# A hybrid mLSTM/attention backbone on one core: the norm's modulated input, its Newton step, its residual, and z in wide matmuls

## The chip, the core and the metric

The kernel runs on one core of a Trainium2 chip. The time is the device time of one execution in microseconds (us). The core's engines have queues of their own and run side by side: TensorE (PE in the profile; PEld are its weight loads), VectorE (DVE), ScalarE (ACT), GpSimd (POOL) and SyncE (SP, which here issues DMAs). Within a queue the order is that of the program; between queues semaphores make an instruction wait for its operands. SBUF is the memory on the chip, PSUM the memory into which TensorE writes.

## What is computed

Two layers over 512 tokens (256 context tokens, then 256 latent ones) of width 1024. Each layer is FFN, token mixer (mLSTM in layer 0, windowed attention in layer 1), FFN. Each of the six sub-layers takes an input that is modulated by a scale and a shift from a conditioning vector, and is followed by a LayerNorm of the weighted sum of the residual and the gated output:

```python
def layer_norm(x, g, b):
    mu = xf.mean(-1, keepdims=True)
    var = jnp.mean(jnp.square(xf - mu), -1, keepdims=True)
    return (xf - mu) * lax.rsqrt(var + LN_EPS) * g + b
def modulate(s, m, slot):
    return s * (1 + m[..., 3 * slot + 1, :]) + m[..., 3 * slot, :]
def residual_post_norm(s, y, gate, weight, g, b):
    return layer_norm(ALPHA * s + weight * gate * y, g, b)
...
xm, z = jnp.split(u @ w_up, 2, axis=-1)         # mLSTM: u is 512 x 1024, z is 512 x 2048
h = jax.nn.sigmoid(z) * h                       # the gate on the mLSTM's output
```

Everything is fp32 in and out.

## The kernel before, in words

*Products.* A product of two fp32 matrices is made of three TensorE products of a high and a low part: each operand is split into `hi`, its rounding to the matmul's own type, and `lo`, what is left, and `mm3` adds hi·hi, hi·lo and lo·hi in PSUM. Weights come from HBM as raw fp32 tiles of 1 MB and less; ScalarE rounds them (`w`, L375) and VectorE or GpSimd subtracts (L376). The sub-layer's input is kept as `uh` and `ul`, eight tiles of 128 features x 512 tokens each.

*Layout.* The residual is `as`, eight SBUF tiles of 128 features x 512 tokens. The tokens are two halves: C0 (columns 0 to 255) and C1 (256 to 511).

*The norm between two sub-layers.* While a sub-layer's output is evicted (L761: `as = y*gate + as`), `Norm.add` accumulates the sum and the sum of squares (`acc`, L107 and L108). `Norm.finish` runs once a half: small matmuls against ones give mean and mean square (`stat`); variance plus epsilon goes through GpSimd's pow and one Newton step (L138 to L141, `rsqrt`, L794 to L799: `ln` tiles of 128x2); GpSimd subtracts the mean from the eight `as` tiles (L145); TensorE spreads the 1/sigma of each token over all partitions into a PSUM tile `rstd`; VectorE multiplies each `as` tile by it in place (L168); `modulate` makes `uh` (ScalarE, L566), `uf` (VectorE, L567) and `ul = uf - uh` (VectorE, L568); and GpSimd later turns `as` into the next residual, scale and shift by `ag` (L174). `Norm` with two halves runs four times: FFN to mLSTM (the first norm, from about 390 us), mLSTM to FFN (the second, from about 810), FFN of layer 0 to FFN of layer 1 (the third, from about 1196) and FFN to attention (the fourth, from about 1573). It runs once with one half, attention to the last FFN (from about 1720). The norm after the last FFN is another class and stays as it is.

*z.* In the mLSTM, z is made with tokens on the partitions: for each of eight column blocks `q` of 256, `tok_major` runs, for each of four tiles of 128 tokens, eight feature tiles x 3 matmuls of 128x128 by 128x256. Two token tiles share a PSUM tile of 128x512, which ScalarE evicts with a tanh (L951) and which is then stored.

*What sets the order.* TensorE's and SyncE's orders are written out by a planner: tasks are generators that yield a delay or an event, `drive` always runs the first task that is due on a clock `k.T`, which matmuls advance by their modelled time. Its constants (LAT, SOLO, RY in ns) say how long after one step of the norm the next is put into the program: LAT[0] and LAT[1] before the statistics of the first and second half, LAT[2] (SOLO with one half) between statistics and `rstd`, LAT[3] and LAT[4] from `rstd` to the first use of `u`, RY from the modulated input to the residual's rescale. VectorE's, ScalarE's and GpSimd's orders come from a scheduler, in which `high_priority` moves an instruction forward.

## Time and profile before

| | |
|---|---|
| median of 3 runs | 1941.97 us (1941.0 to 1946.05) |
| the profiled execution's own time | 1937.41 us |
| its span, first to last instruction | 1935.6 us |
| mean granted TensorE clock | 0.989 |
| TensorE busy | 1881.0 us, 97 % |
| VectorE, ScalarE, GpSimd busy | 69 %, 42 %, 19 % |
| z matmuls (128x256) | 768 |

How to read the rows that follow. A row of a group reads: line, engine, operation, written tile <- read tiles, shape, count | busy us in all, mean ns of one | idle us of the engine just before them, and what ended most of it. A row of a timeline reads: start us, us, engine, line, operation, tiles, count, and in brackets the idle time before it and what ended that. A row of the waits reads: waiting engine, its tile and line <- the engine, tile and line that ended the wait: us in all, times, longest. A row of the chain reads: start, us, engine, tile, line, count. A row of windows reads: window, its length, then PE, PEld, DVE, ACT and POOL busy with counts, then the granted TensorE clock, the DMA share and GB/s.

### The profile page before, as it was taken

How to read it: one execution, taken by the hardware profiler on the slowest of the kernel's cores; microseconds unless marked ns; L12 is line 12 of the kernel's file. 1: busy time of each engine (PE TensorE's matmuls, PEld its weight loads, DVE VectorE, ACT ScalarE, POOL GpSimd, SP SyncE). 2: the span in 40 equal slices, each digit the busy share in tenths (PEclk: the TensorE clock that was granted, in tenths of full speed). 3: DMA queues.
4: the chain of work that ended last, by engine and by line, in shares of the span. 5: the costliest groups of instructions: out<-in, count | busy, mean ns of one | idle time of the engine just before them, and what ended most of it. 6: DMA issues, size and time to landing. Idle time of an engine off the chain costs nothing.

```text
span 1935.6 us, 28837 instructions
## 1 busy us (share of the span) xinstructions
PE 1881.0 (97%) x10946; PEld 1610.6 (83%) x10946; DVE 1339.4 (69%) x2424; ACT 819.3 (42%) x1521; POOL 366.6 (19%) x397
## 2 busy tenths in 40 slices
PE   7999999999999999989999999999999999989997
PEld 5888888897889977978888889888888888789997
DVE  4976677986664689777776679776633468966565
ACT  3443233246555563343323333433233335745452
POOL 2000000570012344450000025400000256140000
PEclk9999999999999999999999999999999999999999
DMA  9654454435343464335455434454432224126652
GB/s 318 218 203 166 153 194 160 136 120 185 96 150 115 134 215 142 109 116 182 154 180 174 158 136 142 148 185 147 152 107 87 94 69 131 45 66 198 194 164 99
DMA packets 227435, 287.55 MB, mean 149 GB/s; under 512 B 7968, under 2 KB 197536, under 8 KB 227296
## 3 DMA queue, kind: packets, MB, share of 16 engines
q1 hardware_dynamic: 226384, 282.75, 44.1%
q0 software_dynamic: 912, 2.95, 0.4%
q8 instruction: 86, 1.41, 0.3%
q14 instruction: 53, 0.43, 0.1%
HBM read 269.94 MB, written 15.73 MB: 148 GB/s over the span
## 4 chain that ended last, share of the span: by engine, by line
PE 56%; DVE 3%; POOL 1%; issue 1%; ACT 1%; DVEq 0%; POOLq 0%; ACTq 0%
PE gv L294 31%; PE y L294 19%; PE q L294 1%; PE s L294 1%; DVE ul L568 1%; PE o L294 1%; PE stat L294 0%; DVE uf L567 0%; PE pT L301 0%; PE msum L294 0%; PE h L294 0%; POOL as L145 0%; DVE as L168 0%; ACT e L1386 0%; PE swap L294 0%
## 5 line engine op out<-in xcount | busy, mean ns | idle before, releaser
L294 PE MATMUL gv<-uh,w 128*128 128x512 f32 (+1 forms) x2944 | 799.7, 358 | 11.5 <-DVE w L376 5.5
L375 ACT ACTIVATE w<-raw 128x512 fp32r<-128x512 f32 x636 | 395.7, 630 | 692.7 <-PE gv L294 395.6
L376 DVE TENSOR_TENSOR w<-raw,w 128x512 fp32r<-128x512 f32 x604 | 433.7, 723 | 299.1 <-ACT w L375 296.9
L294 PEld LDWEIGHTS gv<-uh,w 128*128 128x128 f32 x2944 | 527.1, 191 | 97.9 <-DVE w L376 5.7
L294 PE MATMUL gv<-ul,w 128*128 128x512 f32 (+1 forms) x1472 | 525.1, 357 | 1.8 <-DVE ul L568 1.8
L294 PE MATMUL y<-hh,w 128*128 128x512 f32 (+1 forms) x1600 | 405.6, 342 | 0.0
L493 DVE SCALAR_TENSOR_TENSOR macc<-mraw,cs,macc 128x512 f32<-128x512 f32 x448 | 331.7, 785 | 41.0 <-DMA mraw<-in_mod_w 32.0
L294 PEld LDWEIGHTS gv<-ul,w 128*128 128x128 f32 x1472 | 281.0, 191 | 40.5 <-DVE ul L568 2.4
L294 PEld LDWEIGHTS y<-hh,w 128*128 128x128 f32 x1600 | 277.9, 190 | 37.7 <-issue 3.2
L294 PE MATMUL y<-hl,w 128*128 128x512 f32 (+1 forms) x800 | 272.2, 340 | 0.0
L88 POOL TENSOR_TENSOR as<-as,shift 128x512 f32<-128x512 f32 (+1 forms) x40 | 57.6, 1475 | 889.0 <-ACT shift L86 889.0
L294 PEld LDWEIGHTS y<-hl,w 128*128 128x128 f32 x800 | 151.7, 190 | 17.6 <-issue 0.7
L761 DVE SCALAR_TENSOR_TENSOR as<-y,gate,as 128x256 f32<-128x256 f32 x184 | 78.9, 476 | 36.3 <-PE y L294 36.2
L294 PE MATMUL z<-w,uh 128*128 128x256 f32 x512 | 94.1, 285 | 0.0
L294 PE MATMUL xm<-uh,w 128*128 128x512 f32 (+1 forms) x320 | 91.3, 359 | 0.0
L677 DVE TENSOR_TENSOR sg<-sg,gv 128x512 f32<-128x512 f32 (+1 forms) x88 | 54.0, 618 | 52.9 <-PE gv L294 48.5
L294 PE MATMUL y<-hnh,w 128*128 128x512 f32 (+1 forms) x320 | 85.2, 350 | 0.7 <-DVE as L761 0.7
L376 POOL TENSOR_TENSOR w<-raw,w 128x512 fp32r<-128x512 f32 x32 | 45.7, 1429 | 201.9 <-ACT w L375 194.0
L294 PEld LDWEIGHTS z<-w,uh 128*128 128x128 f32 x512 | 79.8, 191 | 2.5 <-issue 2.1
L294 PE MATMUL z<-w,ul 128*128 128x256 f32 x256 | 72.4, 283 | 0.0
L294 PEld LDWEIGHTS xm<-uh,w 128*128 128x128 f32 x320 | 57.8, 195 | 12.2 <-issue 5.0
L558 ACT ACTIVATE hh<-sg 128x512 fp32r<-128x512 f32 (+1 forms) x88 | 50.3, 575 | 37.0 <-DVE sg L677 37.0
(298 smaller groups left out, 2279.3 us busy)
## 6 DMA issues: line engine op xcount, KB each, us to landing
raw<-in_ffn_w_in SPq DMA_DIRECT2D x84, 1024.0 KB, 5.2
mraw<-in_mod_w SPq DMA_DIRECT2D x128, 512.0 KB, 6.1
raw<-in_ffn_w_out SPq DMA_DIRECT2D x48, 768.0 KB, 4.6
raw<-in_ml_w_up SPq DMA_DIRECT2D x15, 1024.0 KB, 5.8
m<-in_mod_w SPq DMA_DIRECT2D x32, 256.0 KB, 6.6
raw<-in_ffn_w_out SPq DMA_DIRECT2D x16, 512.0 KB, 3.4
raw<-in_ml_w_down SPq DMA_DIRECT2D x16, 512.0 KB, 3.9
raw<-in_at_w_qkv SPq DMA_DIRECT2D x6, 1024.0 KB, 5.1
```

The source lines that it names most:

```text
L88: nc.gpsimd.tensor_tensor(out=k.as_[d][:, cols], in0=k.as_[d][:, cols], in1=sh[:, cols], op=ALU.subtract)
L294: k.nc.tensor.matmul(out, lhsT=lhsT, rhs=rhs, start=start, stop=stop, skip_group_check=True, **kw)
L375: k.nc.scalar.activation(h, view, AF.Copy)
L376: (k.nc.gpsimd if pool else k.nc.vector).tensor_tensor(out=l, in0=view, in1=h.bitcast(F32), op=ALU.subtract)
L493: V.scalar_tensor_tensor(out=o, in0=r, scalar=cf, in1=o, op0=ALU.mult, op1=ALU.add)
L558: k.nc.scalar.activation(hi[:, cols], src, AF.Copy)
L568: nc.vector.tensor_tensor(out=u[1][:, cs], in0=f[:, cs], in1=u[0][:, cs].bitcast(F32), op=ALU.subtract)
L677: nc.vector.tensor_tensor(out=sg[:, cols], in0=sg[:, cols], in1=gv[1][:, cols], op=ALU.mult)
L761: nc.vector.scalar_tensor_tensor(out=k.as_[d][:, cs], in0=ys[dp][e][:, cs], scalar=G[:, d, c:c + 1], in1=k.as_[d][:, cs], op0=ALU.mult, op ...
```

## The change

Four parts.

1. Variance and Newton step: one VectorE operation makes variance plus epsilon straight from `stat`, pow stays on GpSimd, the Newton step is three VectorE operations. LAT[2] goes from 3000 to 2600, SOLO from 2000 to 1800.
2. Modulated input: `uf = as*A*rstd` in one VectorE operation from the centred `as` and PSUM, `uh` from it on ScalarE with the shift as bias, `ul = (uf + B) - uh` in one VectorE operation. Two VectorE operations a tile, where there were three; `as` stays centred.
3. Residual: ScalarE copies `rstd` to SBUF, and after RY (20000, was 14000) GpSimd multiplies `as` by it (new) and then scales and shifts as before.
4. z: four column blocks of 512, one token tile to a PSUM tile, 128x128 by 128x512 matmuls; the passes over a block's weights are token tile 0, tile 1, then 2 and 3 together. The weights are loaded and split in another arrangement (`plan_wide`), in as many loads and splits of the same size.

```diff
-LAT = (1700, 3500, 3000, 2000, 2200)
-SOLO, RY, ST, LT = 2000, 14000, 2500, 1500
+LAT = (1700, 3500, 2600, 2000, 2200)
+SOLO, RY, ST, LT = 1800, 20000, 2500, 1500
@@ Norm.finish
             nc.scalar.activation(w[0], st[:, o:o + 2], AF.Square)
-            nc.scalar.activation(w[1], st[:, o + 2:o + 4], AF.Copy, bias=EPS)
-            P.tensor_tensor(out=w[1], in0=w[1], in1=w[0], op=ALU.subtract)
-            y = k.rsqrt(w[1], w[2], w[3], True)
+            V.scalar_tensor_tensor(out=w[1], in0=st[:, o + 2:o + 4], scalar=EPS, in1=w[0], op0=ALU.add, op1=ALU.subtract)
+            y, t = w[2], w[3]
+            P.tensor_tensor(out=y, in0=w[1], in1=k.mhalf[:, 0:2], op=ALU.pow)
+            V.scalar_tensor_tensor(out=t, in0=w[1], scalar=-0.5, in1=y, op0=ALU.mult, op1=ALU.mult)
+            V.tensor_tensor(out=t, in0=t, in1=y, op=ALU.mult)
+            V.scalar_tensor_tensor(out=y, in0=t, scalar=1.5, in1=y, op0=ALU.add, op1=ALU.mult)
...
         for d in range(KD):
-            r = k.as_[d][:, cs]
-            nc.vector.tensor_tensor(out=r, in0=r, in1=y, op=ALU.mult)
-            A, B = s.AB
-            k.modulate(r, A[:, d, c:c + 1], B[:, d, c:c + 1], cs, s.u[d])
+            f = k.a(name="uf")
+            bd = B[:, d, c:c + 1]
+            nc.vector.scalar_tensor_tensor(out=f[:, cs], in0=k.as_[d][:, cs], scalar=A[:, d, c:c + 1], in1=bc[:, cs], op0=ALU.mult, op1=ALU.mult)
+            hi, lo = s.u[d]
+            nc.scalar.activation(hi[:, cs], f[:, cs], AF.Identity, bias=bd)
+            nc.vector.scalar_tensor_tensor(out=lo[:, cs], in0=f[:, cs], scalar=bd, in1=hi[:, cs].bitcast(F32), op0=ALU.add, op1=ALU.subtract)
+            k.free(f)
+        rs = k.a(name="rstd")
+        nc.scalar.activation(rs[:, cs], bc[:, cs], AF.Copy)
         yield RY
         for d in range(KD):
             r = k.as_[d][:, cs]
-            nc.gpsimd.tensor_scalar(out=r, in0=r, scalar1=s.ag[:, 0, d:d + 1], scalar2=s.ag[:, 1, d:d + 1], op0=ALU.mult, op1=ALU.add)
+            P.tensor_tensor(out=r, in0=r, in1=rs[:, cs], op=ALU.mult)
+            P.tensor_scalar(out=r, in0=r, scalar1=s.ag[:, 0, d:d + 1], scalar2=s.ag[:, 1, d:d + 1], op0=ALU.mult, op1=ALU.add)
+        k.free(rs)
@@ the weights of z, and z
-        for q in range(8):
-            k.plan_tokmaj(("z", q), w, 2048 + q * 256, ZP)
+        for q in range(4):
+            k.plan_wide(("z", q), w, 2048 + q * 512, ZP)
...
-        for q in range(8):
-            pc = yield from k.need(("z", q))
-            for tp in range(2):
-                p = k.ps("z")
-                for th in range(2):
-                    tok = slice((2 * tp + th) * 128, (2 * tp + th + 1) * 128)
-                    yield from k.tok_major(p[:, th * 256:(th + 1) * 256], u, tok, pc, th == 0)
+        for q in range(4):
+            for ts in ((0,), (1,), (2, 3)):
+                ps = [k.ps("z") for _ in ts]
+                for t in range(KD):
+                    w = yield from k.need(("z", q, t))
+                    wh, wl = w[0][:, 0], w[1][:, 0]
+                    for tt, p in zip(ts, ps):
+                        tok = slice(tt * 128, tt * 128 + 128)
+                        uh, ul = u[t][0][:, tok], u[t][1][:, tok]
+                        k.mm(p, uh, wh, t == 0, False)
+                        k.mm(p, uh, wl, False, False)
+                        k.mm(p, ul, wh, False, t == KD - 1)
+                        yield 0
+                    if ts[-1] == 3:
+                        k.done(("z", q, t))
```

The diff doesn't show what the scheduler makes of it. Line numbers of the changed kernel are its own (L389 is the old L376, L781 the old L761). GpSimd in the fourth norm, at the second half's pow; before (L794 is the pow, L145 the subtracts, L174 the scales):

```order
L108 TENSOR_TENSOR acc_13919<-acc_13919,sq 128x256
L1301 DMA swap<-in_swap 128x128
L174 TENSOR_SCALAR as<-as,ag 128x256 x8
L140 TENSOR_TENSOR ln<-ln 128x2
L794 TENSOR_TENSOR ln<-ln,mhalf 128x2
```

and in the change (L143 is the pow, L150 the subtracts, L185 the new multiplication, L186 the scale):

```order
L1319 DMA swap<-in_swap 128x128
L185 TENSOR_TENSOR as<-as,rstd 128x256 x2
L186 TENSOR_SCALAR as<-as,ag 128x256 x2
L185 TENSOR_TENSOR as<-as,rstd 128x256 x2
L186 TENSOR_SCALAR as<-as,ag 128x256 x2
L143 TENSOR_TENSOR ln<-ln,mhalf 128x2
L185 TENSOR_TENSOR as<-as,rstd 128x256 x2
L150 TENSOR_TENSOR as<-as,acc_13534 128x256 x8
```

Eight scales of the first half stood ahead of the pow; now four multiplications and four scales do, and two multiplications more ahead of the subtracts. In the second norm all sixteen stand ahead of it, in the first and third three.

VectorE in the second norm, between the first half's modulated input and the weight split behind it; before:

```order
L567 TENSOR_SCALAR uf<-as,cAA,cAB 128x256
L107 TENSOR_TENSOR acc_7511<-acc_7511,as 128x256
L568 TENSOR_TENSOR ul_8061<-uf,uh_8060 128x256
L107 TENSOR_TENSOR acc_7511<-acc_7511,as 128x256
L761 SCALAR_TENSOR_TENSOR as<-y,gate_6682,as 128x256 x2
L107 TENSOR_TENSOR acc_7511<-acc_7511,as 128x256
L376 TENSOR_TENSOR w<-raw,w 128x512
```

and in the change:

```order
L175 SCALAR_TENSOR_TENSOR uf<-as,cAA,rstd 128x256
L178 SCALAR_TENSOR_TENSOR ul_7673<-uf,cAB,uh_7672 128x256
L107 TENSOR_TENSOR acc_7127<-acc_7127,as 128x256
L178 SCALAR_TENSOR_TENSOR ul_7675<-uf,cAB,uh_7674 128x256
L107 TENSOR_TENSOR acc_7127<-acc_7127,as 128x256
L781 SCALAR_TENSOR_TENSOR as<-y,gate_6297,as 128x256 x2
L107 TENSOR_TENSOR acc_7127<-acc_7127,as 128x256
L389 TENSOR_TENSOR w<-raw,w 128x512
```

From the half's first L168 (before) or L175 (change) up to this split there were 31 VectorE operations, and there are 23 now.

GpSimd in the same norm, behind the first half's pow; in the change:

```order
L143 TENSOR_TENSOR ln<-ln,mhalf 128x2
L150 TENSOR_TENSOR as<-as,acc_7127 128x256 x8
L108 TENSOR_TENSOR acc_7128<-acc_7128,sq 128x256 x3
L185 TENSOR_TENSOR as<-as,rstd 128x256 x2
L186 TENSOR_SCALAR as<-as,ag 128x256 x2
```

Between the pow and the subtracts stood the four Newton operations L796 to L799; they are on VectorE now, and GpSimd goes straight on.

More of the change, by code (lines that the diff above doesn't have):

```diff
@@ L392, in plan_tokmaj, with plan_wide, load @@
         k.plan_raw(load, [(name, 8, lambda r: [k.split(r.rearrange("p (a b) -> p a b", a=8)[:, 2 * a:2 * a + 2, :], 2, a in pool) for a in range(4)])])
+    def plan_wide(k, name, w, c0, pool=()):
+        for half in range(2):
+            def load(r, half=half):
+                k.nc.sync.dma_start(r.rearrange("p (a b) -> p a b", a=4), w[half * 512:(half + 1) * 512, c0:c0 + 512].rearrange("(a p) c -> p a c", p=128))
+            k.plan_raw(load, [(name + (4 * half + a,), 2, lambda r, a=a: k.split(r.rearrange("p (a b) -> p a b", a=4)[:, a:a + 1, :], 1, a in pool)) for a in range(4)])
     def plan_up(k, l, j, ms):
@@ L906, in key_xm @@
         return ("xm", j, 0) if j in (0, 2, 3) else ("xm", 0, 1) if j == 1 else ("xm", j - j % 2, j % 2)
-    def tok_major(k, o, u, tok, pc, first):
-        for t in range(KD):
-            w = (pc[t // 2][0][:, t % 2], pc[t // 2][1][:, t % 2])
-            uh, ul = u[t][0][:, tok], u[t][1][:, tok]
-            k.mm(o, uh, w[0], t == 0 and first, False)
-            k.mm(o, uh, w[1], False, False)
-            k.mm(o, ul, w[0], False, t == KD - 1)
-            yield 0
     def g_ml_main(k, norm, G, mk_norm):
@@ L942, in g_ml_main @@
             k.spawn(k.g_head(h), 5)
-        for q in range(8):
-            pc = yield from k.need(("z", q))
-            for tp in range(2):
-                p = k.ps("z")
-                for th in range(2):
-                    tok = slice((2 * tp + th) * 128, (2 * tp + th + 1) * 128)
-                    yield from k.tok_major(p[:, th * 256:(th + 1) * 256], u, tok, pc, th == 0)
-                zt = k.a(name="zt")
-                k.nc.scalar.activation(zt, p, AF.Tanh, scale=0.5)
-                k.spawn(k.store(k.zs[2 * tp:2 * tp + 2, :, q * 256:(q + 1) * 256].rearrange("t p c -> p t c"),
-                                zt.rearrange("p (t c) -> p t c", t=2), zt, k.z_ev[q // 2] if q % 2 and tp else None), 1)
-            k.done(("z", q))
+        for q in range(4):
[13 more added lines that the diff above has]
+                        k.done(("z", q, t))
+                for tt, p in zip(ts, ps):
+                    zt = k.a(name="zt")
+                    k.nc.scalar.activation(zt, p, AF.Tanh, scale=0.5)
+                    k.spawn(k.store(k.zs[tt, :, q * 512:(q + 1) * 512], zt, zt, k.z_ev[q] if tt == 3 else None), 1)
         k.free(u)
```

3 lines of the change are left out of this document (2 added, 1 removed).

## The prediction

> **What bounds the kernel now.** The page first: which engine is never idle, and who carries the chain of work that ended last.
>
> ```profile
> span 1935.6 us, 28837 instructions
> PE 1881.0 (97%) x10946; PEld 1610.6 (83%) x10946; DVE 1339.4 (69%) x2424; ACT 819.3 (42%) x1521; POOL 366.6 (19%) x397
> ```
>
> TensorE works 97 % of the span. So there are two ways to gain: fewer or quicker TensorE instructions, or less of the 54.6 us (1935.6 − 1881.0) in which it waits. The list of waits, for TensorE alone, says who makes it wait (columns: total us, times, longest):
>
> ```profile
> PE gv L294 <- DVE w L376: 5.5, 1, 5.5
> PE stat L294 <- DVE acc L107: 4.5, 3, 1.7
> PE rstd L294 <- POOL ln L799: 3.5, 2, 1.9
> PE gv L294 <- DVE as L761: 2.0, 1, 2.0
> PE gv L294 <- DVE ul L568: 1.8, 2, 1.5
> PE k L294 <- DVE ul L568: 0.7, 2, 0.5
> ```
>
> These rows, 18 us, lie nearly all in the five places where a `Norm` runs between two sub-layers; the other idle time lies at the start, in the mLSTM heads and in attention, which the change leaves alone. Three rows name VectorE work that stands in a queue with the norm's own operations, one names GpSimd's Newton step. The largest place is the second norm (mLSTM to FFN). Its timeline, TensorE and VectorE, and the windows around it:
>
> ```profile
> 825.76 0.39 PE L294 MATMUL gv<-uh,w 128*128 128x256 f32 x1 [1.97 <-DVE as L761]
> ...
> 831.76 0.80 PE L294 MATMUL gv<-uh,w 128*128 128x256 f32 x2 [5.50 <-DVE w L376]
> ```
>
> ```profile
> 817.05 0.97 DVE L168 TENSOR_TENSOR as<-as,rstd 128x256 f32<-128x256 f32 x2
> ...
> 831.03 0.68 DVE L376 TENSOR_TENSOR w<-raw,w 128x512 fp32r<-128x512 f32 x1
> ```
>
> ```profile
> 828.00:832.00 4.00, 0.24 (x1) 0.24 (x2) 3.58 (x10) 1.41 (x3) 4.00 (x5) 0.50 0.01 2
> 832.00:836.00 4.00, 3.89 (x22) 3.68 (x22) 2.41 (x7) 0.00 (x0) 1.48 (x3) 0.68 0.00 0
> ```
>
> TensorE stands 7.5 us for the VectorE queue; the weight split at 831.03 had 31 operations between it and 817.05. The windows (the eighth column is the granted clock) show a clock of 0.50 and then 0.68: a stall here is followed by slow matmuls, some 1.3 us in those 4 us ((1 − 0.68) × 4).
>
> **z (part 4).** It halves the matmuls, 768 of 256 columns to 384 of 512, with the same arithmetic.
>
> ```profile
> L294 PE MATMUL z<-w,uh 128*128 128x256 f32 x512 | 94.1, 285 | 0.0
> L294 PE MATMUL z<-w,ul 128*128 128x256 f32 x256 | 72.4, 283 | 0.0
> ```
>
> ```profile
> 1416.43 108.80 PE gv L294 x480
> ...
> 1836.27 57.60 PE gv L294 x480
> ```
>
> The durations overlap, so the pace comes from two chain rows of 480 matmuls in one unbroken run: 57.60/480 = 120.0 ns (256 columns) and 108.80/480 = 226.7 ns (512 columns). 768 × 0.1200 = 92.2 us becomes 384 × 0.2267 = 87.1: **−5.1 us**. The stage has no idle time (0.0 in both rows), so all of it counts. Bounds: 0, if z's pace is set by something else there, and −5.1. I take −5.1.
>
> The Trainium skill ("TensorE: Matmul & The Clock Gate", section "Wait — 56ns, not 53.3ns?") puts a fixed gap of about 2.5 ns on each matmul; by it 384 fewer would be worth some 1.0 us, an estimate from that page. The two chain rows give a fixed part of 2 × 120.0 − 226.7 = 13.3 ns, so the trace does not agree, and its number is used.
>
> The splits (32), the 1 MB loads (8), the stores (16) and the tanh evictions (16) stay as many; z's own first pass over a token tile takes a weight item per 3 matmuls (0.68 us) where a VectorE split takes 0.68 us (row at 831.03): level, with stock ahead. Costed at nothing; if the stock is out, some tenths of a microsecond a q.
>
> **Modulation in two VectorE operations (part 2).**
>
> ```profile
> L168 DVE TENSOR_TENSOR as<-as,rstd 128x256 f32<-128x256 f32 x72 | 27.7, 410 | 15.1 <-PE rstd L294 13.6 <-POOL as L145 0.9
> L567 DVE TENSOR_SCALAR uf<-as,cBA,cBB 128x256 f32<-128x256 f32 x40 | 21.8, 578 | 1.4 <-POOL acc L108 1.4
> L568 DVE TENSOR_TENSOR ul<-uf,uh 128x256 fp32r<-128x256 f32 x88 | 46.8, 558 | 1.7 <-ACT uh L566 1.4
> ```
>
> The new `uf` reads the same tile and the same PSUM tile as L168 and takes its 0.41; the new `ul` has L568's operands and takes its 0.56. ScalarE's `uh` keeps its shape and is waited for nowhere here. So L567 goes: 0.58 × 8 = 4.6 us a half norm, 72 × 0.58 = 42 us of VectorE. It is worth something on TensorE only where VectorE ends a wait. In the second norm the split that TensorE waits for now follows 23 operations, not 31 (order above), mean (831.03 − 817.05)/31 = 0.45: −8 × 0.45 = **−3.6 us** of that stall. In the first, third and fourth norms the wait for `acc` (4.5 in three, 1.5 each) stands behind the same work and is covered by 4.6 less.
>
> **Newton on VectorE (part 1).** Today, second norm, first half, and a VectorE operation of the new kind beside a GpSimd one:
>
> ```profile
> 813.06 0.20 POOL L140 TENSOR_TENSOR ln<-ln 128x2 f32<-128x2 f32 x1 [4.29 <-ACT ln L139]
> 813.33 0.71 POOL L794 TENSOR_TENSOR ln<-ln,mhalf 128x2 f32<-128x2 f32 x1
> ...
> 815.51 0.68 POOL L799 TENSOR_TENSOR ln<-ln 128x2 f32<-128x2 f32 x1
> ```
>
> ```profile
> 779.16 1.32 POOL L376 TENSOR_TENSOR w<-raw,w 128x512 fp32r<-128x512 f32 x1
> 779.25 1.25 DVE L801 SCALAR_TENSOR_TENSOR rsn<-ve,rsn 128x4 f32<-128x4 f32 x1 [2.23 <-POOL rsn L794]
> 780.54 0.16 DVE L802 TENSOR_TENSOR rsn<-rsn 128x4 f32<-128x4 f32 x1
> ```
>
> The chain is 3.1 us now (813.06 to 816.19). The new one is best 0.16 + 0.71 + 3 × 0.16 and three hand-overs of about 0.05: 1.5 us. But L801 shows the price beside GpSimd: a 128x4 operation that takes 0.16 alone took 1.25, ending as the GpSimd operation that began before it ended (780.48). In the order of the change GpSimd goes from the pow straight to its subtracts (0.76 each, 6.06/8 below), so each of the three may wait for one: 0.2 + 0.7 + 3 × 0.8 = 3.3 us. Between 1.5 and 3.3 against 2.1 to 3.1 before: −1.0 to +1.2 a half; I take +0.3 in each of the four first halves, **+1.2 us**, since the subtracts do follow at once.
>
> The Trainium skill ("SBUF — State Buffer", section "Who interferes with whom") says that a VectorE instruction with two SBUF inputs contends with a GpSimd one that reads SBUF, that the one issued first holds the shared ports for the whole instruction, and that one with a single SBUF input is free of it. The trace agrees: 1.25 against 0.16 here, and L168, with one SBUF input, stays at 0.41 while L568 means 0.56. By that rule alone the three Newton operations would take the 3.3 us, and the term would be 4 × 1.2 = 4.8 us, not 1.2, and the forecast 1941, still no change that can be told.
>
> **The residual later (part 3).** Removed: L168's write of the normalised `as`. Added on GpSimd: 72 multiplications with the copied `rstd`, which can't start before the copy, which stands on ScalarE behind the eighth `uh`. Price by the nearest row, L145 (same shape, two SBUF inputs):
>
> ```profile
> 824.89 7.16 POOL L174 TENSOR_SCALAR as<-as,ag 128x256 f32<-128x256 f32 x8
> ...
> 1593.45 1.62 POOL L174 TENSOR_SCALAR as<-as,ag 128x256 f32<-128x256 f32 x1 [0.32 <-DVE uf L567]
> 1595.05 0.19 POOL L140 TENSOR_TENSOR ln<-ln 128x2 f32<-128x2 f32 x1
> 1595.32 1.05 POOL L794 TENSOR_TENSOR ln<-ln,mhalf 128x2 f32<-128x2 f32 x1
> ...
> 1597.43 6.06 POOL L145 TENSOR_TENSOR as<-as,acc 128x256 f32<-128x256 f32 x8
> ```
>
> ```profile
> 1597.54 0.71 PE L294 MATMUL rstd<-ident,ln 128*128 128x128 f32 x4 [1.89 <-POOL ln L799]
> ```
>
> ```profile
> 1592.71 0.57 DVE L567 TENSOR_SCALAR uf<-as,cAA,cAB 128x256 f32<-128x256 f32 x1
> ```
>
> 72 × 0.76 = 55 us of GpSimd, which is 19 % busy. What counts is who stands behind them: the pow of the second half. In the fourth norm it already waits for the scales of the first (the last, 1.62 long, ends at 1595.07) and costs TensorE 1.89 us. Now 8 rescale operations stand ahead of it, all behind the copy. The last `uf` ends at 1593.28 now; with eight L567 less, 4.6 us, and two operations re-ordered, about 1589.5; `uh` and copy, 0.6 + 0.4, so 1590.5; then 4 × 0.76 + 4 × 0.7 (between 0.55 and 0.90, 7.16/8) = 5.8: the pow at about 1596.3 against 1595.32, and `rstd` ready 0.7 + 0.8 to 2.4 behind that, 1597.8 to 1599.4 against 1597.5. **+1.5 us**, bounds −3 (copy early, no wait left) and +5.5 (copy where the last `uf` is now).
>
> In the second norm all 16 stand ahead. From about 827.5 (copy), with two accumulations between: 8 × 0.76 + 8 × (0.55 to 0.90) + 1.5 = 12 to 15 us, 839.5 to 842.5; `rstd` ready 2 us later, 841.5 to 844.5. Before:
>
> ```profile
> 838.23 0.71 POOL L794 TENSOR_TENSOR ln<-ln,mhalf 128x2 f32<-128x2 f32 x1
> ```
>
> ```profile
> 841.74 0.42 DVE L168 TENSOR_TENSOR as<-as,rstd 128x256 f32<-128x256 f32 x1 [3.97 <-PE rstd L294]
> ```
>
> So the 3.6 us won on the split are lost again to `rstd`, and up to 3 more: net **+1.0**, bounds −5 and +5. In the first and third norms only three stand ahead, and 2 us earlier work pays for them:
>
> ```profile
> 408.08 1.87 PE L294 MATMUL stat<-ones,acc 128*128 128x1 f32 x8 [1.68 <-DVE acc L107]
> ```
>
> ```profile
> 411.95 1.03 POOL L794 TENSOR_TENSOR ln<-ln,mhalf 128x2 f32<-128x2 f32 x1
> ```
>
> pow ran 3.9 us after the statistics began to run; with the copy near 407 and three operations it starts at 409.5 or so. I take the `acc` wait as won: **−1.5 each**, bounds −3 and +2.5. In the norm before the last FFN there is one half and nothing ahead of the pow; its wait for `ul` (1.5) goes, the one for Newton stays: **−1.2**, bounds −3 and +1.
>
> RY 14000 to 20000 also moves nine xm matmuls of 512 columns behind `v`, 2 us less cover there: **+0.5**, bounds 0 and +2.
>
> **Sum.** −5.1 − 1.5 + 1.0 − 1.5 + 1.5 − 1.2 + 1.2 + 0.5 = −5.1. The profiled execution took 1937.4 us (span 1935.6 and 1.8 around it), so 1932.3 in its own terms. That execution was 4.6 us quicker than the median of the runs, 1942.0, and quicker than each of them. The same difference on the median gives 1936.9; I predict **1937 us**.
>
> **Rivals.**
> - *The relief reaches TensorE everywhere.* The copy comes early enough, GpSimd uses its idle time, and the stalls of the table that VectorE ends go with the slow clock behind them. For it: GpSimd is idle 81 % of the span, and VectorE was busy 3.58 of 4 us in the window at 828 while TensorE stood. Against it: 16 rescale operations ahead of one pow. Time: −5.1 − 1.5 × 3 − 5.0 (second norm) − 2.0 (fourth and last) − 1.3 for the clock = −18, halved in its norm part for what cannot all go: −11.5, 1930.
> - *The rescale decides (the other side).* Place: GpSimd's queue ahead of the second half's pow. From the point where copy plus operations ahead end after the time at which TensorE needs `rstd` (841.5 and 1597.5 in the second and fourth norms), every microsecond counts, and the slow clock behind it. Upper bounds: 2.5 + 5 + 2.5 + 5.5, with 1.3 for the clock twice, 0.3 × 4 for Newton, −5.1 for z: +14, 1956; a middle is +9, 1951. For it: pow already waits there today. Against it: the copy moves forward with VectorE.
> - *z saves nothing*, because the weights' splits or the evictions pace it: the sum without it is 0, 1942.
>
> **How the numbers follow.** What one measurement of this kernel can tell from no change is about 0.3 %, 5.8 us: 1936.1 to 1947.8. Forecast 0.40 (its own range 1932 to 1943), relief 0.32, rescale 0.18, z for nothing 0.10. Faster: most of the relief (0.29) and a quarter of the forecast (0.10), 0.39. Slower: the rescale (0.16) and some of the rest (0.03), 0.19. Same: 0.42. Range: from 1926 (relief with more of its full −18) to 1951 (the middle of the rescale).
>
> **What would show it.** z right: 384 z matmuls at a pace of 227 ns, no idle before them. Modulation: the wait of `gv` for `w` at 2 us or gone, `acc` waits gone. Newton: the three VectorE operations at 0.16 or near 0.8. Rescale: the wait of TensorE for `ln` above 3.5 us in total, its longest in the second and fourth norms, with L185 and L186 right ahead of L143 on GpSimd. The prediction fails if `ln` ends no wait (then the relief holds), or if it ends more than 8 us.

## The result, and the profile after

The changed kernel takes 1985.64 us (median of 4 runs, 1984.94 to 1988.67); the kernel before, beside it, takes 1941.49 (1939.53 to 1946.05). The ratio is 1.0233, with a 95 % interval of 1.0215 to 1.0251: 44 us slower, outside the predicted range of 1926 to 1951. The profiled execution has a span of 1986.8 us and a mean granted clock of 0.975 (before 1935.6 and 0.989).

The page of the changed kernel, its span and its engines:

```profile
span 1986.8 us, 27926 instructions
PE 1889.4 (95%) x10562; PEld 1599.3 (80%) x10562; DVE 1342.3 (68%) x2388; ACT 812.4 (41%) x1521; POOL 409.9 (21%) x424
```

No engine became the bound: VectorE has as much work as before and GpSimd 43 us more, on an engine that is still idle four fifths of the span. What grew is the time in which TensorE waits. Its list of waits (line numbers are the changed kernel's: L307 is the matmul, L389 the weight split, L146 the last Newton operation):

```profile
PE rstd L307 <- DVE ln L146: 19.4, 6, 13.6
PE mtp L314 <- ACT macc L524: 19.1, 3, 11.5
PE gv L307 <- DVE w L389: 13.6, 1, 13.6
...
PE h L307 <- ACT vh L578: 3.5, 1, 3.5
PE stat L307 <- DVE acc L108: 1.4, 3, 0.5
```

Four stalls stand out: one of 13.6 for `rstd`, one of 13.6 for a split `w`, two of 11.5 and 7.5 for `mtp` (the transpose of a modulation vector, which no step of the prediction touched). Together they are 46.2 us. Where they lie is seen from the start of the first statistics matmul of each norm, read off TensorE's timeline of each profiled execution; `z_only` is the kernel before with the z part alone (below):

| us from norm to norm | before | z_only | after |
|---|---|---|---|
| start to first | 391.5 | 392.4 | 393.8 |
| first to second (norm, mLSTM) | 419.7 | 415.2 | 432.3 |
| second to third (norm, FFN) | 385.1 | 385.6 | 403.8 |
| third to fourth (norm, FFN) | 376.7 | 376.7 | 378.2 |
| fourth to last (norm, attention) | 147.4 | 149.0 | 163.7 |
| last to end | 215.2 | 215.2 | 215.1 |

Against z_only the change loses 17.1, 18.2 and 14.7 us behind the first, second and fourth norm, and next to nothing elsewhere.

**Behind the first norm**, VectorE stands at an instruction that no step of the prediction named: L92, which fills `ag`, the residual's scale and shift of a later norm, into a ring of two tiles. Its tile comes free when the last rescale of an earlier norm has read it. VectorE's timeline of the changed kernel, then GpSimd's (the first two rows begin the run of rescale operations, the last two end it), then TensorE's:

```profile
444.03 0.25 DVE L92 TENSOR_SCALAR ag<-par 128x8 f32<-128x8 f32 x2 [13.55 <-POOL as L186]
...
448.87 0.69 DVE L908 TENSOR_TENSOR bm<-mqkh,cst 128x512 fp32r<-128x512 f32 x1 [3.40 <-DMA rs<-as]
```

```profile
425.32 1.60 POOL L185 TENSOR_TENSOR as<-as,rstd 128x256 f32<-128x256 f32 x2
426.91 3.03 POOL L186 TENSOR_SCALAR as<-as,ag 128x256 f32<-128x256 f32 x2
...
442.88 1.11 POOL L186 TENSOR_SCALAR as<-as,ag 128x256 f32<-128x256 f32 x2
443.92 4.35 POOL L939 DMA_DIRECT2D rs<-as  x8
```

```profile
446.13 1.11 PE L314 MATMUL mtp<-ident,macc 128*128 128x128 f32 x4 [11.47 <-ACT macc L524]
```

GpSimd has no gap from 425.3 to 443.99. VectorE can pass nothing that is queued behind L92, and ScalarE stands behind VectorE: its L1005 waits for a copy (L1004) queued behind L92, and the `macc` that `mtp` reads is queued behind L1005. So TensorE runs out too.

```profile
444.90 0.69 ACT L1005 ACTIVATE xc<-xm,par 128x512 f32<-128x512 f32 x1 [11.95 <-DVE xm L1004]
445.49 0.59 ACT L524 ACTIVATE macc<-msum 128x512 f32<-128x512 f32 x1
```

The windows of the changed kernel show VectorE, GpSimd and TensorE (columns: PE, PEld, DVE, ACT, POOL, granted clock, DMA share, GB/s):

```profile
430.00:440.00 10.00, 4.66 (x38) 3.48 (x36) 0.48 (x1) 0.63 (x1) 9.89 (x16) 0.93 0.30 97
440.00:450.00 10.00, 2.82 (x12) 2.53 (x12) 2.57 (x6) 2.21 (x4) 8.27 (x15) 0.50 0.47 169
450.00:460.00 10.00, 9.07 (x38) 7.53 (x38) 8.63 (x15) 8.30 (x15) 0.00 (x0) 0.72 0.74 263
```

GpSimd is busy 9.89 of 10 us while VectorE is busy 0.48; behind the stall the clock stays at 0.72 for a whole window. Before, the same instruction on VectorE waited too, but for a rescale without multiplications, and 1.72 us instead of 13.55:

```profile
433.30 0.25 DVE L92 TENSOR_SCALAR ag<-par 128x8 f32<-128x8 f32 x2 [1.72 <-POOL as L174]
```

**Behind the second norm**, VectorE again, and the GpSimd operations that it waits for (L108 adds squares for the second half's statistics, and runs on both engines):

```profile
850.29 2.17 DVE L108 TENSOR_TENSOR acc<-acc,sq 128x256 f32<-128x256 f32 x1 [5.35 <-POOL acc L108]
...
853.67 3.22 DVE L389 TENSOR_TENSOR w<-raw,w 128x512 fp32r<-128x512 f32 x4
```

```profile
841.89 1.84 POOL L185 TENSOR_TENSOR as<-as,rstd 128x256 f32<-128x256 f32 x2 [3.53 <-ACT rstd L181]
...
847.63 0.73 POOL L108 TENSOR_TENSOR acc<-acc,sq 128x256 f32<-128x256 f32 x1
...
849.53 0.73 POOL L108 TENSOR_TENSOR acc<-acc,sq 128x256 f32<-128x256 f32 x1
...
860.85 0.71 POOL L143 TENSOR_TENSOR ln<-ln,mhalf 128x2 f32<-128x2 f32 x1 [3.61 <-DVE ln L141]
```

Seven rescale operations run ahead of the first of these L108 and nine ahead of the second. VectorE's own L108 waits for the second; the split that TensorE needs stands behind that on VectorE, and TensorE stands 13.6 us. The kernel before already had this wait, 1.88 us long, behind eight scales:

```profile
833.59 0.43 DVE L108 TENSOR_TENSOR acc<-acc,sq 128x256 f32<-128x256 f32 x1 [1.88 <-POOL acc L108]
```

The pow (L143), which the prediction watched, sat idle for 3.61 us and waited for VectorE, not for the rescale. The loss goes on in the FFN: L92 holds VectorE for another 8.27 us at 888, and the other `mtp` wait (7.46 us) comes at 935.8.

**Behind the fourth norm**, GpSimd and then VectorE, in the second half:

```profile
1632.04 0.72 POOL L143 TENSOR_TENSOR ln<-ln,mhalf 128x2 f32<-128x2 f32 x1
1632.75 1.39 POOL L185 TENSOR_TENSOR as<-as,rstd 128x256 f32<-128x256 f32 x2
1634.11 5.47 POOL L150 TENSOR_TENSOR as<-as,acc 128x256 f32<-128x256 f32 x8
```

```profile
1628.24 0.15 DVE L141 SCALAR_TENSOR_TENSOR ln<-stat,ln 128x2 f32<-128x2 f32 x1
1632.79 6.81 DVE L144 SCALAR_TENSOR_TENSOR ln<-ln 128x2 f32<-128x2 f32 x1 [3.59 <-POOL ln L143]
1639.63 0.49 DVE L145 TENSOR_TENSOR ln<-ln 128x2 f32<-128x2 f32 x1
1640.16 1.90 DVE L146 SCALAR_TENSOR_TENSOR ln<-ln 128x2 f32<-128x2 f32 x1
```

The variance is there at 1628.4. The pow starts 3.65 us later, behind eight rescale operations, as the prediction feared. Then the first Newton operation, two elements a partition, takes 6.81 us: it ends at 1639.60, when the unbroken run of ten GpSimd operations (two L185, eight L150) has ended at 1639.58. `rstd` starts at 1642.11 after a wait of 13.56.

A run of subtracts behind the pow does not by itself hold that operation so long. In the second norm's second half eight L150 follow the pow without a gap (861.53, 6.44 us), L144 starts at 861.59, and it takes 0.70 us. Of the nine halves this is the only one in which a multiplication L185 is the first operation behind the pow, and the only one in which L144 is long. It takes 0.68 to 0.70 where a subtract is first (six halves) and 0.16 and 0.19 where a scale L186 is first (two).

### The profile page after: what moved, and what is told of

It is laid out like the page before. It is cut to its first block, busy times and chain, and to the rows that moved or that the text cites. A ratio compares the mean times of both kernels' runs of the same rounds, so it can differ in the third digit from the quotient of the medians.

```text
span 1986.8 us, 27926 instructions
## 1 busy us (share of the span) xinstructions
PE 1889.4 (95%) x10562; PEld 1599.3 (80%) x10562; DVE 1342.3 (68%) x2388; ACT 812.4 (41%) x1521; POOL 409.9 (21%) x424
## 4 chain that ended last, share of the span: by engine, by line
PE 86%; DVE 7%; POOL 3%; ACT 1%; DMA 1%; issue 1%; SPq 0%; DVEq 0%; ACTq 0%; POOLq 0%
PE gv L307 42%; PE y L307 25%; PE z L307 4%; PE xm L307 3%; PE h L307 2%; PE S L307 2%; PE q L307 1%; POOL as L185 1%; PE v L307 1%; DVE w L389 1%; POOL as L186 1%; PE s L307 1%; PE msum L307 1%; DVE uf L175 1%; DVE ul L178 1%
## 5 line engine op out<-in xcount | busy, mean ns | idle before, releaser
L307 PE MATMUL gv<-uh,w 128*128 128x512 f32 (+1 forms) x2944 | 802.4, 359 | 19.0 <-DVE w L389 13.6
L389 DVE TENSOR_TENSOR w<-raw,w 128x512 fp32r<-128x512 f32 x604 | 438.7, 733 | 310.4 <-ACT w L388 304.6
L307 PEld LDWEIGHTS gv<-uh,w 128*128 128x128 f32 x2944 | 529.0, 191 | 105.5 <-DVE w L389 13.8
L307 PE MATMUL gv<-ul,w 128*128 128x512 f32 (+1 forms) x1472 | 526.4, 358 | 0.6 <-DVE ul L178 0.5
L307 PE MATMUL y<-hh,w 128*128 128x512 f32 (+1 forms) x1600 | 405.8, 342 | 0.0
L307 PEld LDWEIGHTS gv<-ul,w 128*128 128x128 f32 x1472 | 281.8, 191 | 39.8 <-DVE ul L178 0.8
L307 PEld LDWEIGHTS y<-hh,w 128*128 128x128 f32 x1600 | 277.9, 190 | 37.9 <-issue 2.4
L307 PE MATMUL y<-hl,w 128*128 128x512 f32 (+1 forms) x800 | 272.2, 340 | 0.0
L307 PEld LDWEIGHTS y<-hl,w 128*128 128x128 f32 x800 | 151.7, 190 | 17.4 <-issue 0.7
L781 DVE SCALAR_TENSOR_TENSOR as<-y,gate,as 128x256 f32<-128x256 f32 x184 | 79.2, 475 | 29.0 <-PE y L307 29.0
L307 PE MATMUL xm<-uh,w 128*128 128x512 f32 (+1 forms) x320 | 90.7, 358 | 0.0
L389 POOL TENSOR_TENSOR w<-raw,w 128x512 fp32r<-128x512 f32 x32 | 45.2, 1413 | 212.7 <-ACT w L388 211.1
L307 PE MATMUL y<-hnh,w 128*128 128x512 f32 (+1 forms) x320 | 85.2, 350 | 0.0
L307 PE MATMUL z<-w,uh 128*128 128x512 f32 x256 | 80.4, 395 | 0.0
L185 POOL TENSOR_TENSOR as<-as,rstd 128x256 f32<-128x256 f32 x72 | 61.5, 875 | 39.2 <-ACT rstd L181 20.9
L307 PEld LDWEIGHTS xm<-uh,w 128*128 128x128 f32 x320 | 57.6, 194 | 12.2 <-issue 5.0
L307 PEld LDWEIGHTS y<-hnh,w 128*128 128x128 f32 x320 | 56.2, 189 | 7.8 <-issue 0.4
```

What stands on the lines that cost most here:

```text
L185: P.tensor_tensor(out=r, in0=r, in1=rs[:, cs], op=ALU.mult)
L307: k.nc.tensor.matmul(out, lhsT=lhsT, rhs=rhs, start=start, stop=stop, skip_group_check=True, **kw)
L389: (k.nc.gpsimd if pool else k.nc.vector).tensor_tensor(out=l, in0=view, in1=h.bitcast(F32), op=ALU.subtract)
L781: nc.vector.scalar_tensor_tensor(out=k.as_[d][:, cs], in0=ys[dp][e][:, cs], scalar=G[:, d, c:c + 1], in1=k.as_[d][:, cs], op0=ALU.mult, op ...
```

## The experiments

In the medians below each group has its own runs of the kernel before (1939.72, 1940.11, 1940.22 and 1939.89 us). Stage lengths are those of the table above, in the same order.

### The parts alone

*z alone.* The kernel before with part 4 of the diff and nothing else.

> The kernel before with part 4 alone (z in 384 matmuls of 512 columns). Pace theory: 384 x (2 x 120.0 - 226.7) ns = 5.1 us less, so about 1936.4 against 1941.5; the z matmuls at 227 ns pace and no idle before them. Rival (weights or evictions pace z): no change, 1941, with TensorE waits at z. If z were the cause of the loss it would be above 1960.

Measured: 1936.34 us, ratio 0.9982 [0.997, 0.9993]. The z matmuls, by their tile, in the kernel before and in this one (ns min/median/max, first and last start):

```profile
L294 PE MATMUL z<-w,uh x512: 277/283/386, 562.6 to 685.1; 128*128 128x256 f32 x171
```

```profile
L294 PE MATMUL z<-w,uh x256: 387/389/500, 563.6 to 681.3; 128*128 128x512 f32 x128
```

Unbroken, they run at the pace that was forecast: 24 of them make one chain row of 5.47 us, 228 ns each. From first to last start it is 117.7 us where it was 122.5, 4.8 less; the stage first to second norm is 4.5 shorter, and the whole 3.4. Behind z, in the heads, a wait of `h` for ScalarE's `vh` grows from 1.1 to 3.6 us. The wide z is a gain, and almost all of what was predicted of it.

*z and the Newton step.* Parts 4 and 1:

```diff
+            V.scalar_tensor_tensor(out=w[1], in0=st[:, o + 2:o + 4], scalar=EPS, in1=w[0], op0=ALU.add, op1=ALU.subtract)
...
+            V.scalar_tensor_tensor(out=y, in0=t, scalar=1.5, in1=y, op0=ALU.add, op1=ALU.mult)
```

> The kernel before with part 4 and part 1 (z wide; variance and Newton on VectorE with LAT 2600 and SOLO 1800), the modulation and the residual as before. Shared-port theory: against z alone (1936.3) up to 1.2 us a half norm slower, 1937 to 1946. Rival: part 1 a gain of 0.5 us or so a half, 1931 to 1936.

Measured: 1939.56, ratio 0.9992 [0.9982, 1.0003]; 3.2 us above z_only by the medians, 1.9 by the ratios, whose intervals overlap. The first Newton operation, by its line, in this kernel:

```profile
L143 DVE SCALAR_TENSOR_TENSOR ln<-ln x9: 160/691/703, 395.2 to 1726.7; 128x2 f32<-128x2 f32 x9
```

Its median is 0.69 us and its longest 0.70: about one GpSimd operation long, since GpSimd goes on to its subtracts at once. The 6.81 us of the changed kernel are not here, where GpSimd has no multiplications in its queue.

*Everything but the multiplications.* The changed kernel without the copy of `rstd` and the 72 multiplications:

```diff
-        rs = k.a(name="rstd")
-        nc.scalar.activation(rs[:, cs], bc[:, cs], AF.Copy)
...
-            P.tensor_tensor(out=r, in0=r, in1=rs[:, cs], op=ALU.mult)
```

> The changed kernel with the copy of rstd and the 72 GpSimd multiplications left out (the residual is then not divided by the standard deviation; all else, Newton on VectorE and two-operation modulation, as changed). Theory (the multiplications on GpSimd make the loss, by its queue and by what waits for the residual): the waits of 11.5 us (mtp), 13.6 (w) and 13.6 (ln) all go, 1932 to 1942. Rival (the changed VectorE work makes it): above 1955.

Measured: 1941.70, ratio 1.001 [1.0, 1.002]. The loss is gone: stages 419.7, 387.7, 377.4 and 147.7. So the multiplications (61.5 us of GpSimd's time) with their copies cost the 44 us: 12.6, 16.1, 0.8 and 16.0 in these stages. What the copies cost by themselves (they take a buffer each) was not run.

The rest of the change, freed of them, is slower than z alone: 1941.7 against 1936.3. Nearly all of this is RY:

```diff
-SOLO, RY, ST, LT = 1800, 20000, 2500, 1500
+SOLO, RY, ST, LT = 1800, 14000, 2500, 1500
```

> The run without the multiplication with RY back at 14000 (the rest as there). Theory (RY moves xm matmuls behind v and costs the first norm's stage 4.5 us against z alone): the stage from the first to the second norm falls from 419.7 to 415 to 416, 1937 to 1938. Rival (Newton and modulation cost it): 419 to 420, 1941 to 1942.

Measured: 1937.48, ratio 0.9982 [0.9972, 0.9993]. RY at 20000 cost 4.2 us by the medians, 5.4 by the ratios; the first stage goes from 419.7 to 413.5, and a wait of 2.7 us for `mtp` is gone.

With RY back the kernel is level with z_only (both ratios 0.9982), so Newton and modulation together are worth nothing that can be told. Why the modulation gains nothing is seen in the second norm. The split that TensorE waits for, VectorE and TensorE in no_multiply (L385 is the split there):

```profile
828.96 1.20 DVE L385 TENSOR_TENSOR w<-raw,w 128x512 fp32r<-128x512 f32 x1
830.77 0.42 DVE L108 TENSOR_TENSOR acc<-acc,sq 128x256 f32<-128x256 f32 x1 [0.61 <-POOL acc L108]
...
832.12 0.68 DVE L385 TENSOR_TENSOR w<-raw,w 128x512 fp32r<-128x512 f32 x1
```

```profile
832.86 0.80 PE L303 MATMUL gv<-uh,w 128*128 128x256 f32 x2 [7.23 <-DVE w L385]
```

TensorE does not start behind the split at 828.96 but behind the one at 832.12. So it needs the second of the two, where in the kernel before it started behind the first. Rows printed without buffer numbers look alike, and the prediction counted up to the wrong one. That the scheduler exchanged two weight pieces is inferred from the wait. With the right one 28 VectorE operations stand ahead, where there were 31, and the wait grew from 5.5 to 7.2 us. They also start later: the first `uf` 7.50 us after the first statistics matmul (810.73 to 818.23), where in z_only the first L168 starts 5.83 us after it (807.66 to 813.49).

### Who waits for GpSimd's rescale

Four edits of the changed kernel: two apart, both together, and a third on top of these. They leave the multiplications in and take away what waits for them.

`ag_five`: the ring of `ag` gets five tiles, so L92 need not wait.

```diff
-        s.ag = k.sp.tile([128, 2, 8], F32, tag="ag", name="ag", bufs=2)
+        s.ag = k.sp.tile([128, 2, 8], F32, tag="ag", name="ag", bufs=5)
```

> The changed kernel with five buffers for ag, not two, so that no later norm's ag waits for an earlier norm's rescale. Ring theory: L92 no longer stands at the head of VectorE's queue (33.5 us in three waits), the 11.5 us wait of mtp in the first norm goes, with the slow clock and the small waits behind it: 14 to 18 us less, about 1969. Rival (GpSimd's queue alone makes the loss): VectorE's wait falls but TensorE's time stays, 1982 to 1986.

Measured: 1977.17, ratio 1.0194 [1.0176, 1.0212]; stages 432.6, 392.5, 379.3, 161.4. It gains about half of the 14 to 18 us expected, and not in the norm for which they were. The second stage gains 11.3 us (the wait for `mtp` in the FFN is gone). The first gains nothing, because a second wait stands a few instructions behind L92 on VectorE's queue:

```profile
447.08 0.69 DVE L908 TENSOR_TENSOR bm<-mqkh,cst 128x512 fp32r<-128x512 f32 x1 [13.94 <-DMA rs<-as]
```

`bm` takes a buffer that `as` gives back once it has been stored, and the store waits for the last rescale. TensorE stands 13.2 us for `xm` instead of 11.5 for `mtp`.

`kept_order`: the rescale stays behind the second half's accumulations, pow and subtracts on GpSimd.

```diff
-            P.tensor_tensor(out=r, in0=r, in1=rs[:, cs], op=ALU.mult)
-            P.tensor_scalar(out=r, ...)
+            k.tc.keep_in_program_order(P.tensor_tensor(out=r, in0=r, in1=rs[:, cs], op=ALU.mult))
+            k.tc.keep_in_program_order(P.tensor_scalar(out=r, ...))
```

> The changed kernel with the rescale (L185, L186) kept in program order with the subtracts, so that the second half's accumulations, pow and subtracts stand ahead of it on GpSimd. Queue theory: the waits of 13.6 us in the second norm (gv for w) and 13.6 us in the fourth (rstd for ln) fall below 5 each, and the 7.5 us behind the second with them: 20 to 30 us less, 1956 to 1966. ag's wait stays or grows. Ring theory alone: 1980 or more.

Measured: 1980.50, ratio 1.0211 [1.0192, 1.023]; stages 431.1, 403.9, 380.2, 156.9. The order does what it was to do: the `rstd` wait in the fourth norm falls from 13.6 to at most 2.1, the pow of the second norm runs at 850.6 instead of 860.9 (with the norm's start 3.6 us earlier), the split's wait falls from 13.6 to 6.9, near the 7.2 that no_multiply has. The time follows by 5 us only, far short of the expected gain: `mtp` makes TensorE wait 20.5 us in three places, another split 4.7 in the FFN behind the second norm, and `shift` 3.7 behind the fourth. The new order puts the rescale later and does not bring its end forward.

`kept_ag_five`: both edits.

> Both: rescale kept in program order and five ag buffers. If queue and ring make all of the loss and are independent: 1985.6 - 16 - 25 = 1945, 1940 to 1950, and with z's 5.1 still in it perhaps below 1941.5. If Newton on VectorE beside GpSimd (L144 up to 6.8 us) is a cause of its own: above 1950 with waits of rstd for ln left, 5 us and more in total.

Measured: 1962.54, ratio 1.0121 [1.0104, 1.0138]; stages 429.9, 389.0, 376.4, 156.7. By the ratios they gain 0.0112 together, some 22 us, and 0.0039 and 0.0022 apart, 12 us in sum: either wait hides part of the other. The time is above 1950, as the expectation's second case has it, and the `rstd` waits that it names are there, 6.3 us. But Newton on VectorE is not what is left (it is tested below): the first stage still has the wait of `bm` (14.29 us on VectorE) and the 12.5 of `mtp`.

`kept_ag_late`: in addition the `as` buffers of the mLSTM are given back later, so that `bm` takes others.

```diff
-        k.free(k.as_)
...
+            if j == 8:
+                k.free(k.as_)
```

> The run with the kept order and five ag buffers, and as freed four xm blocks later in the mLSTM, so that bm and xm no longer take the buffers that GpSimd still has to rescale and store (VectorE's wait of 14.29 us for the store rs<-as). Buffer theory: TensorE's wait of 12.5 us in the first norm (mtp for macc) goes with the slow clock behind it: 1962.5 - 14 to 17, 1945 to 1949. Rival (the rescale's length is waited for by something else, the residual's reuse only came first): the wait stays under another name, above 1957.

Measured: 1953.55, ratio 1.0064 [1.0047, 1.0081]; stages 423.5, 388.5, 376.6, 156.8. The time falls by 9 us by the medians and 11 by the ratios, between the theory (14 to 17) and the rival. The wait of `bm` and the 12.5 us are gone, the first stage is 6.4 us shorter. What is left is mostly in the last of the four, from the fourth norm through attention: 156.8, where no_multiply has 147.7. TensorE in this kernel, in the fourth norm:

```profile
1624.27 1.22 PE L307 MATMUL shift<-as,ones 128*128 128x256 f32 x2 [5.04 <-POOL as L186]
```

`shift` sums the rescaled residual for the sub-layer that follows, so it can't run before the rescale. It waits here because the kept order has put the rescale behind the second half's subtracts, and the rescale now takes two GpSimd operations a tile. In the kernel before and in the changed kernel, where the rescale of the first half runs earlier, it ran without a wait:

```profile
1661.07 0.59 PE L307 MATMUL shift<-as,ones 128*128 128x256 f32 x2
```

(the changed kernel). So the new order trades one wait for another. This one is 5.0 of the 9 us; the rest of this stage, and about 4 us in the first, stay without a single named cause.

### The Newton step beside the rescale

In the changed kernel, and in kept_ag_late, variance and Newton go back to ScalarE and GpSimd:

```diff
-            V.scalar_tensor_tensor(out=w[1], in0=st[:, o + 2:o + 4], scalar=EPS, in1=w[0], op0=ALU.add, op1=ALU.subtract)
...
+            nc.scalar.activation(w[1], st[:, o + 2:o + 4], AF.Copy, bias=EPS)
+            P.tensor_tensor(out=w[1], in0=w[1], in1=w[0], op=ALU.subtract)
+            y = k.rsqrt(w[1], w[2], w[3], True)
```

> The changed kernel with variance and Newton back on GpSimd and ScalarE, all else as changed. Shared-port theory: the 13.6 us wait of rstd in the fourth norm (an operation on 2 elements a lane that took 6.81 us beside ten GpSimd operations) falls to the queue's part, 5 to 8, so 6 to 10 us less, 1976 to 1980. Queue theory alone: the wait stays at 12 to 14, 1984 to 1988.

> The same with the variance and the Newton step back on GpSimd and ScalarE (part 1 undone but for its constants). Shared-port theory: the three VectorE operations beside GpSimd's subtracts cost; without them rstd for ln falls (1.8 + 2.1 + 1.6 us in the kept run) and the time by 1 to 5 us. Rival (Newton on VectorE is as good): equal or 1 to 3 us slower, since GpSimd's own queue grows by 1.1 us a half.

Measured: pool_newton 1983.13, ratio 1.0214 [1.0193, 1.0236]; kept_ag_late_poolnewton 1955.46, 1.0072 [1.0055, 1.009]. In the first, the longest `rstd` wait falls from 13.6 to 6.5 and the stage of the fourth norm from 163.7 to 156.6: there the held VectorE operation was worth 7 us. The whole gains little, between the two expectations: the third to fourth stage grows from 378.2 to 382.2 and the first to second from 432.3 to 433.9, while the second to third gains 2.0. In the second, where the order on GpSimd is mended, the place of Newton makes no difference that the intervals tell apart. So the 6.81 us belong to the order in that half, not to Newton on VectorE as such: in the four runs where Newton is on VectorE and the subtracts alone follow the pow (kept_order, kept_ag_five, kept_ag_late, no_multiply) it never takes more than 0.70. Why a multiplication behind the pow makes it ten operations long and a subtract one stays open.

### The multiplication on VectorE

Not a delayed rescale: VectorE multiplies `as` by `rstd` from PSUM behind the eight `ul`, RY 14000; then the same with Newton back on GpSimd and its old constants.

```diff
-        rs = k.a(name="rstd")
-        nc.scalar.activation(rs[:, cs], bc[:, cs], AF.Copy)
+        for d in range(KD):
+            nc.vector.tensor_tensor(out=k.as_[d][:, cs], in0=k.as_[d][:, cs], in1=bc[:, cs], op=ALU.mult)
...
-            P.tensor_tensor(out=r, in0=r, in1=rs[:, cs], op=ALU.mult)
```

> The changed kernel with the residual's multiplication on VectorE, from PSUM, behind the eight ul of the half (72 x 0.41 us back on VectorE, none on GpSimd, no copy), RY 14000. Theory: the three long waits go; against the run without the multiplication 3.3 us more VectorE work a half, of which 0 to 2 us each show: 1932 to 1946. Rival: VectorE's load is what counts, above 1950.

> The same with variance and Newton on GpSimd and ScalarE as before and LAT 3000, SOLO 2000: of the four parts, z and the two-operation modulation are left, with the multiplication moved behind it on VectorE. Shared-port theory: 1 to 4 us quicker than with Newton on VectorE, and, since u comes earlier, at or below z alone: 1931 to 1938. Rival (no gain from the modulation): 1936 to 1942.

Measured: 1948.69, ratio 1.0038 [1.0026, 1.0051], and 1942.14, 1.0013 [1.0004, 1.0023]. The big loss is gone, but so is any gain over z alone: VectorE has again three operations a tile, and the wait of `gv` for the split is 10.2 us in both. The first lies between its theory and its rival, the second at the upper end of its rival.

### The split first

If VectorE's order were all that is wrong in the second norm, putting the weight split ahead would win the wait. One constant, in z_only, no_multiply and multiply_on_vector_pool_newton:

```diff
-        with k.tc.high_priority(offset=-200 if k.calm.t is None else 0):
+        with k.tc.high_priority(offset=100 if k.calm.t is None else 0):
```

> The kernel before with part 4, and the weight splits inside the norms at a higher scheduler priority (+100 for -200), so that in the second norm the split that TensorE waits for stands ahead of the first half's u on VectorE, not 31 operations behind it. Theory (that split's place in VectorE's queue makes the 5.25 + 1.98 us wait): the wait goes, u comes 0.6 us later, 1936.3 - 4 to 7, 1929 to 1933. Rival (u is the bound, the split only came last): the wait turns into one for uh or ul of like length, 1935 to 1938.

> The run without the residual's multiplication and the copy (the residual is not divided by the standard deviation), with the same priority of the weight splits. Theory (in the changed order the split needed first stands behind two accumulations that wait for GpSimd, so the eight operations saved came to nothing): its wait of 7.23 us goes, 1941.7 - 5 to 8, 1934 to 1937. Rival (Newton and the slower uf are what costs): 1939 to 1942.

> Two-operation modulation, the multiplication behind it on VectorE, Newton on GpSimd, z wide, and the weight splits at the higher priority. Theory: the 10.2 us wait for the split in the second norm goes, 1942.1 - 6 to 10, 1932 to 1936. Rival: a wait for u or for acc takes its place, 1939 to 1942.

Measured: 1946.60, ratio 1.003 [1.0019, 1.0041] (z_only 0.9982); 1946.19, 1.0029 [1.0017, 1.004] (no_multiply 1.001); 1940.17, 0.9999 [0.9987, 1.001] (1.0013). The first two are slower than any of their expectations; the third gains 2 us, with intervals that overlap, where 6 to 10 were expected. The wait for `w` in the second norm is gone in all three, and one for `acc` stands in its place: 6.7 us where it was 5.2, 4.7 where it was 7.2, and 10.3 where it was 10.2. TensorE in z_and_weight_first:

```profile
837.47 1.87 PE L294 MATMUL stat<-ones,acc 128*128 128x1 f32 x8 [6.73 <-DVE acc L107]
```

The theory that a better place in the queue wins 4 to 7 us falls: in this norm the place in the queue chooses which of VectorE's operations TensorE waits for. That VectorE simply has more to do there than TensorE has cover for fits this, but is argued. The constant moves the splits of all norms, so the three totals are not the price of the second norm alone (in z_and_weight_first the third to fourth stage grows from 376.7 to 380.7).

No kernel of the study that computes the whole norm beats z_only, which is 3.4 us (0.07 to 0.3 %) better than the kernel before.

## Why the prediction was wrong, step by step

- **z, −5.1: right.** Alone it shortens its stage by 4.5 us and the whole by 3.4, at the pace of 228 ns that was named as its sign. The rival that z saves nothing is out.
- **The residual later: the step that failed.** It said of the multiplications "What counts is who stands behind them: the pow of the second half." In the second norm the pow did not wait for them at all. Others did: L92's ring, with `bm`'s buffer next in line (first norm, 12.6 us), the accumulations L108 and L92 again (second norm, 16.1), and the pow together with a Newton operation on VectorE (fourth norm, 16.0, of which the Newton operation 7). The queue itself was reckoned nearly right. The sixteen rescale operations and two accumulations of the second norm took 15.4 us (841.89 to 857.24) where 12 to 15 were forecast, and the pow of the fourth norm's second half started 24.05 us after the norm's first statistics (1607.99 to 1632.04) where 23.3 was forecast (1573.0 to 1596.3). What was wrong is who waits. The prediction even priced those accumulations ("with two accumulations between", 1.5 us) as time ahead of the pow, and did not ask who waits for them. Its rows for the first, second and fourth norm, −1.5, +1.0 and +1.5, measured +17.1, +18.2 and +14.7 against z_only, with whatever the other parts do there (no_multiply keeps 4.5 of the 17.1). For the third and last it said −1.5 and −1.2; measured +1.5 and 0.
- **The price of the multiplications: nearly right.** 55 us were forecast from L145's 0.76; they took 61.5. GpSimd's 19 % share stands beside that price as if it were room. It was the wrong number: behind the first norm GpSimd is full (9.89 of 10 us), and there are things that wait for the end of its rescale.
- **Modulation, −3.6 on the split: wrong.** The count of 23 operations ran to a split that TensorE does not wait for; the right one lost 1.7 us. The waits for `acc`, 4.5 before, fell to 2.4 (1.4 + 1.0): that part held, and was lost in the rest.
- **Newton, +1.2: not told apart from nothing.** Alone it is 1.9 us by the two ratios, whose intervals allow some 3 us either way, and no_multiply_ry shows no loss. The bound behind the term failed: at most 0.8 was allowed for each of the three operations, so 2.4, and in the fourth norm's second half they took 9.3 (1632.79 to 1642.06). Elsewhere it held: their medians are 0.69, 0.38 and 0.67 in the changed kernel, and only the first ever reached 0.16. By the Trainium skill's rule ("SBUF — State Buffer", section "Who interferes with whom") the prediction would have said +4.8. The ratios cannot tell that from +1.2 either.
- **RY, +0.5: mis-sized.** 4.2 us in the kernel without the multiplications, beyond its bound of 2.
- **The rival "The rescale decides"** had the right engine, and the right place in the fourth norm; its bound of +14 was worked out for one waiter, the pow. The signs it named came: `ln` ends 19.4 us of waits, above the 8 at which the prediction was to fail.
- **The forecast and the relief rival** both rested on 42 us less of VectorE's work. Its busy time went from 1339.4 to 1342.3. The groups of VectorE in the changed kernel that answer to L168, L567 and L568, and its first Newton operation:

```profile
L178 DVE SCALAR_TENSOR_TENSOR ul<-uf,cBB,uh 128x256 fp32r<-128x256 f32 x40 | 25.2, 662 | 0.6 <-ACT uh L177 0.6
L178 DVE SCALAR_TENSOR_TENSOR ul<-uf,cAB,uh 128x256 fp32r<-128x256 f32 x32 | 17.4, 572 | 1.6 <-ACT uh L177 1.6
L175 DVE SCALAR_TENSOR_TENSOR uf<-as,cBA,rstd 128x256 f32<-128x256 f32 x40 | 17.1, 469 | 1.8 <-PE rstd L307 1.8
L175 DVE SCALAR_TENSOR_TENSOR uf<-as,cAA,rstd 128x256 f32<-128x256 f32 x32 | 13.8, 469 | 1.4 <-PE rstd L307 1.4
L144 DVE SCALAR_TENSOR_TENSOR ln<-ln 128x2 f32<-128x2 f32 x9 | 11.3, 1257 | 11.8 <-POOL ln L143 11.8
```

The new `uf` takes 0.469 where 0.41 was taken over from L168, the new `ul` 0.57 to 0.66 where it was 0.56. The two make 73.5 us, and the three operations of before 107.4 (27.7 + 39.1 + 40.6, L568's 46.8 without the 16 outside the norms, 6.2 in the changed kernel): 34 us saved, not 42. Newton and variance take 23.5 of them back (11.3 + 4.4 + 6.4 + 1.4). The rest goes to other VectorE operations, among them the 604 splits, 438.7 us where they took 433.7, and the accumulations, 33.6 where they took 30.0. That they are slower beside a busier GpSimd was not tested.

What stays open: what held the Newton operation through ten GpSimd operations; what the copies of `rstd` cost alone; that the copies are what moves `bm` onto a buffer of `as` (argued from the order in which buffers are given back, and only consistent with kept_ag_late); and some 8 us of the remainder in kept_ag_late.

## What to carry to other kernels

Before work is moved to an idle engine, list every instruction, on any engine, that waits for the last of the moved work: readers of its result, writers that reuse its inputs' buffers (small rings above all), and the engine's own operations that are queued behind it; then look at that engine's share within the stage, not over the span. A wait at the head of a queue costs everything behind it, so a tile of 128x16 numbers with two buffers can stop TensorE (7.5 us in the FFN behind the second norm, gone with five buffers). And where several waits share one cause, removing one shows only the next: take away the cause first, to see the whole price, and the waits afterwards.
